# Sums between the stages of a two-layer block moved onto TensorE, and pools opened before the squares

## The chip, the cores and the metric

One core of one Trainium2 chip runs the kernel. The metric is the time of one execution on the device, in microseconds (us). TensorE is called PE here, VectorE DVE, ScalarE ACT, GpSimd POOL and SyncE SP, as the profile calls them.

## The reference

Block 1 (a delta-net and convolution mixer, a mixture of experts) makes a residual stream `x` of 512 tokens by 1024 features. Block 2 takes it through two layers; the change lies there. A layer of block 2 ends its two halves alike:

```python
    y = jnp.concatenate([y_a, y_b, y_c, y_d], axis=-1) @ w_out
    x = x + gate1 * rms_norm(y, attn_post_g)

    h = rms_norm(x, mlp_pre_g) * (1.0 + scale2) + shift2
    y = jnp.square(jax.nn.relu(h @ mlp_w1)) @ mlp_w2
    return x + gate2 * rms_norm(y, mlp_post_g)
```

So at the end of each half of a layer there is a matrix product `y`, an RMS norm of `y`, an addition to `x`, and an RMS norm of the new `x`, whose scaled copy is what the next stage multiplies with its weights. The last half of the last layer has no next stage.

## The kernel before

Tiles are stored with features on the 128 partitions (8 feature tiles, k = 0 to 7) and tokens along the free axis. Matrix products are made at nearly fp32 precision from split operands: `split` writes a high part (`wh`, `lhh`, `ffh`: a cast on ACT, L314) and a low part (`wl`, `lhl`, `ffl`: a subtraction on POOL or DVE, L315), and `mm3` multiplies wh by the high part (L343), wh by the low part (L347) and wl by the high part (L348). One output tile of 128 features over 512 tokens is 24 such matmuls.

A list scheduler orders the instructions of each engine, by the order of the program's text, by priorities and by explicit "issue after" hints. Each engine then runs its own queue strictly in that order, and tile pools decide when memory comes free.

There are four places like the one in the reference. They are called A (layer 0, attention: output projection, some 1690 to 1825 us), B (layer 0, end of the MLP, 2140 to 2210), C (layer 1, attention, 2570 to 2712) and D (layer 1, end of the MLP, 2984 to 3064.6, the end of the kernel).

At A and C the heads of the last mixer are normed (PE L1736, ACT L1737, L1739, PE L1742, a chain of small DVE instructions, ACT `hol` L1747, PE L1750, DVE L1752, POOL L1754), once for each of two tiles m0 and m1, and split. Then the output projection runs: the first four output tiles (m0 to m3) together over 512 tokens, 96 matmuls, with k outermost in the order 0, 1, 4, 5, 6, 7, 2, 3; then `halves` makes the last four tiles (m4 to m7) in two token halves of 256, called a0 to a3 and b0 to b3, 24 matmuls each. B and D use `halves` in the same way for the last four tiles of the second MLP product.

The class `Between` does what follows a place. `add(k, s)` squares an output tile (ACT L2357), squares it times the gain G (ACT L2359), multiplies output, gain and `x` (DVE L2360), and adds each of the three into an accumulator `ba` (DVE L2364). `sums` sums the accumulator over the partitions with six small fp32 matmuls (L2372; D has only one of the three sums, so two), and works out two reciprocal roots on DVE. `finish` spreads them over the partitions (PE L2391), updates `x`, and makes the next stage's split input (ACT L484 `lhh` and its low part). The sums of token half a are taken while half b still runs. That is possible because the next norm's sum is expanded into the three sums and `own_squares`, the sum of squares of the old `x`: eight squares on ACT (L2241, L2243), seven adds on POOL (L2244), four matmuls (L2247).

Before, `own_squares` has a pool of its own, `osq`, opened and closed before the pools of the output projection:

```python
        with ExitStack() as e3:
            self.own_squares(self.pool("osq", es=e3, side=here), "ab")
        ...
        hlE = self.pool("hlE", bufs=2, es=es2, side=here)
```

`hlE`, which holds the split weights of output tiles m1 and m3, lies on the memory of `osq`.

Of the kernel before, what the change touches and what calls it, by code (L numbers as in the profile page):

```python
# [9 lines left out]
F32 = mybir.dt.float32  # L10
# [4 lines left out]
AF = mybir.ActivationFunctionType  # L15
OP = mybir.AluOpType
# [4 lines left out]
P = 128  # L21
T = 512
NT = 4
D = 1024
KD = 8
TC = 256
EPS = 1e-6
# [5 lines left out]
HT = 256  # L33
# [178 lines left out]
def halves(ap, i):  # L212

    return ap.rearrange("p (t i) -> p t i", i=P)[:, HALF[i]]


class Kern:
# [123 lines left out]
    def mm3(self, out, wh, wl, xh, xl, first, last):  # L341
        mm = self.nc.tensor.matmul
        i = mm(out, wh, xh, start=first, stop=False)  # L343
        if self.behind:

            self.tc.add_manual_dep(self.behind.pop().ins, i.ins.name, mybir.DependencyInfo(mybir.DependencyClass.NoSync, mybir.DependencyReason.DATA), reason="order")
        mm(out, wh, xl, start=False, stop=False)  # L347
        mm(out, wl, xh, start=False, stop=last)  # L348

    def mtile(self, w, c0, act, n=T, m=P, tag=None, ks=range(KD)):  # L350

# [1744 lines left out]
    def layer(self, l):  # L2096

        nc, I = self.nc, self.I
        mod = self.mod2[l]
        vec = lambda n, q=8: self.V(n, l * 8, q)  # L2100
        A2, G1, G2 = (self.tab.tile([P, KD], F32, name="%s_%d" % (n, l)) for n in ("lA2", "lG1", "lG2"))
# [10 lines left out]
        here, there = ("right", None) if l else (None, "right")  # L2112
# [6 lines left out]
        for tag, side, name, gi, run in (  # L2119
# [17 lines left out]
                nc.scalar.dma_start(self.x, self.xd)  # L2137
            with ExitStack() as e3:
                run(self.pool(name, es=e3, side=side), out(gi))
        with ExitStack() as e3:  # L2140
            self.own_squares(self.pool("osq", es=e3, side=here), "ab")
        self.step_ = 1
        nc.vector.tensor_mul(G1, mod[:, 16:24], vec("attn_post_g_2"))
        nc.vector.scalar_tensor_tensor(A2, mod[:, 32:40], 1.0, vec("mlp_pre_g_2"), op0=OP.add, op1=OP.mult)
# [5 lines left out]
        self.hl, self.nhl = [self.hlC, hlE, self.hlC, hlE, self.hlC], 0  # L2150
        bd = self.pool("bd", es=es2, side=here)
        b2 = self.pool("lay4", es=es2, side=here)
        o = self.yf
        order = (0, 1, 4, 5, 6, 7, 2, 3)
        for k in order:
            self.split(self.h[0][:, k], self.h[1][:, k], self.yf[:, k])
        ws = [self.chunk(I["w_out_2"][l], j * 256, 256) for j in range(2)]
        for k, p in enumerate(self.mtiles([(w[m], 0, P, None) for w in ws for m in range(2)], self.h, ks=order)):
            nc.scalar.copy(o[:, k], p)
        ws = [self.chunk(I["w_out_2"][l], j * 256, 256) for j in range(2, 4)]  # L2160
        self.subs = (nc.gpsimd,)
        self.halves(ws, self.h, o, nc.scalar.copy, Between(self, o, G1, bd, A2, mod[:, 24:32]), order)

        if l == 0:
            ring = self.pool("mraw", bufs=1, es=es2, side=here)
# [1 line left out]
        for g in range(4):  # L2167
            if l == 0 and g == 2:
                with self.tc.issue_after(relu.ins):
                    self.own_squares(self.lay2, ("hoq", "hol"))  # L2170
            f = [[b2.tile([P, T], F32R, tag=n, name=n, bufs=8) for _ in range(KD)] for n in ("ffh", "ffl")]
            for js in ((0,), (1,), (2,), (3,)) if g else ((0, 1), (2,), (3,)):
                j = js[0]
                ws = [self.chunk(I["mlp_w1_2"][l], g * D + q * 256, 256) for q in js]
                specs = [(w[m], 0, P, None) for w in ws for m in range(2)]
                if g == 0 and j == 2:
                    self.subs = (nc.gpsimd, nc.vector)
                if g or j:
                    ps = self.mtiles(specs, self.h)
                else:  # L2180
                    ps = [self.ps() for _ in specs]
                    for s in (0, HT):
                        self.mtiles(specs, self.h, HT, o=s, ps=ps)
                for i, p in enumerate(ps):
                    r = self.lay2.tile([P, T], F32, tag="rpx", name="ffr", bufs=2)
                    relu = nc.scalar.activation(r, p, AF.Relu)
                    nc.gpsimd.tensor_mul(r, r, r)
                    self.split(f[0][2 * j + i], f[1][2 * j + i], r)
            if l == 0 and g == 0:
                self.step_ = 2  # L2190
                self.pend = self.mods(0, range(5 * D, 6 * D, P), [ring] * 8, 1) + self.mods(1, range(0, MODS_1 * 256, P), [ring] * 48, 1)
            for j in range(4 if g < 3 else 2):
                w = self.chunk(I["mlp_w2_2"][l], g * D + j * 256, 256)
                for i, p in enumerate(self.mtiles([(w[m], 0, P, None) for m in range(2)], f)):
                    k = 2 * j + i
                    if g == 0:
                        nc.scalar.copy(o[:, k], p)
                    else:
                        nc.vector.tensor_add(o[:, k], o[:, k], p)
        ws = [self.chunk(I["mlp_w2_2"][l], g * D + j * 256, 256) for j in range(2, 4)]  # L2200
# [3 lines left out]
        self.halves(ws, f, o, lambda d, p: nc.vector.tensor_add(d, d, p), Between(self, o, G2, bd, *nxt))  # L2204
        es2.close()

    def halves(self, ws, act, o, put, bt, ks=range(KD)):

        ws = [w for q in ws for w in q]

        def tile(i, s):
            p = self.ps()[:, :HT]
            for k in ks:
                x = [h[k] if isinstance(h, list) else h[:, k] for h in act]
                self.mm3(p, ws[i][0][:, k], ws[i][1][:, k], x[0][:, s], x[1][:, s], k == ks[0], k == ks[-1])
            put(o[:, 4 + i, s], p)
            bt.add(4 + i, s)

        a, b = slice(0, HT), slice(HT, T)
        for k in range(4):  # L2220
            bt.add(k, slice(0, T))
        for i in range(4):
            tile(i, a)
        for i in range(4):
            tile(i, b)
            if i == SUMS:
                bt.sums(a)
        bt.finish(a)
        bt.sums(b)
        bt.finish(b)  # L2230

# [2 lines left out]
        self.nc.vector.scalar_tensor_tensor(A, self.mod2[l][:, 8:16], 1.0, self.V("attn_pre_g_2", l * 8, 8), op0=OP.add, op1=OP.mult)  # L2234
        return A

    def own_squares(self, pool, tags):

        nc = self.nc
        acc, sq = (pool.tile([P, T], F32, tag=q, name="os" + q, bufs=1) for q in tags)  # L2240
        nc.scalar.activation(acc, self.x[:, 0], AF.Square)  # L2241
        for k in range(1, KD):
            nc.scalar.activation(sq, self.x[:, k], AF.Square)  # L2243
            nc.gpsimd.tensor_add(acc, acc, sq)  # L2244
        p = self.ps((P, NT), tag="m")
        for t in range(NT):
            nc.tensor.matmul(p[:, t:t + 1], acc[:, t * P:(t + 1) * P], self.ones1, start=True, stop=True)  # L2247
        self.sx = self.tab.tile([P, NT], F32, tag="sx", name="sx", bufs=1)
        nc.vector.tensor_scalar(self.sx, p, 1.0 / D, EPS, op0=OP.mult, op1=OP.add)

    def arrive(self):

# [88 lines left out]
class Between:  # L2341


    def __init__(self, K, o, G, pool, A=None, B=None):
        self.K, self.o, self.G, self.A, self.B, self.pool = K, o, G, A, B, pool
        self.n = 3 if A is not None else 1
        self.acc = pool.tile([P, 3, T], F32, tag="ba", name="ba", bufs=1)
        self.r = {}

    def add(self, k, s):  # L2350

        K, nc, lay, G = self.K, self.K.nc, self.K.lay2, self.G[:, k:k + 1]
        o = self.o[:, k, s]
        dst = [self.acc[:, i, s] for i in range(self.n)]
        if k:
            dst = [lay.tile([P, T], F32, tag=t, name="bs", bufs=b)[:, s] for t, b in ((("rpt", 2), ("rpt", 2), ("rpx", 2)) if k % 2 else (("hoq", 1), ("hol", 1), ("rpx", 2)))[:self.n]]
        nc.scalar.activation(dst[0], o, AF.Square)  # L2357
        if self.n > 1:
            nc.scalar.activation(dst[1], o, AF.Square, scale=G)  # L2359
            nc.vector.scalar_tensor_tensor(dst[2], o, G, K.x[:, k, s], op0=OP.mult, op1=OP.mult)  # L2360
        if k:
            for i, d in enumerate(dst):
                a = self.acc[:, i, s]
                nc.vector.tensor_add(a, a, d)  # L2364

    def sums(self, s):
        K, nc = self.K, self.K.nc
        n = HT // P
        p = K.ps((P, 3, n), tag="m")
        for i in range(self.n):  # L2370
            for t in range(n):
                m = nc.tensor.matmul(p[:, i, t:t + 1], self.acc[:, i, s.start + t * P:s.start + t * P + P], K.ones1, start=True, stop=True)  # L2372
                if s.start and not i and not t and self.A is not None:
                    K.held = [m]
        v, u = (self.pool.tile([P, n], F32, tag="b" + q, name="b" + q, bufs=2) for q in "vu")
        nc.vector.tensor_scalar(v, p[:, 0], 1.0 / D, EPS, op0=OP.mult, op1=OP.add)
        r = K.rsqrt(v, self.pool, "rm%d" % s.start)
        self.r[s.start] = [r]
        if self.A is not None:
            nc.vector.tensor_mul(u, p[:, 1], r)  # L2380
            nc.vector.scalar_tensor_tensor(u, p[:, 2], 2.0, u, op0=OP.mult, op1=OP.add)
            nc.vector.tensor_mul(u, u, r)
            nc.vector.scalar_tensor_tensor(u, u, 1.0 / D, K.sx[:, s.start // P:s.start // P + n], op0=OP.mult, op1=OP.add)
            self.r[s.start].append(K.rsqrt(u, self.pool, "rn%d" % s.start))
# [46 lines left out]
```

## Time and profile before

| | us |
|---|---|
| median of 3 runs | 3070.9 (3060.8 to 3076.36) |
| the profiled execution | 3066.41 |
| its span in the trace | 3064.6 |
| PE busy | 2738.4 (89% of the span) |
| DVE busy | 1516.2 (49%) |
| ACT busy | 934.5 (30%) |
| POOL busy | 1035.9 (34%) |

PE is busy for most of the span, and its mean granted clock is 0.92 of full speed. The four places make up a small part of the span; the change touches nothing outside them. How long something takes there is read from the timeline and the stretches, what PE waits for from the waits.

### The profile page before, as it was taken

The page shows a single profiled execution, that of the slowest core. Times are in us where ns is not written, and L with a number is a line of the kernel's source. Part 1 is how long each engine was busy: PE and PEld are TensorE (multiplying, and loading weights), DVE is VectorE, ACT ScalarE, POOL GpSimd, SP SyncE. Part 2 cuts the span into 40 slices and gives each one's busy share as a digit, 9 for nine tenths or more (in the row PEclk, how much of TensorE's full clock was granted, in tenths as well). Part 3 has the DMA queues.
Part 4 walks back from the last instruction along what each step waited for, and adds up shares of the span by engine and source line. Part 5 has one row for each costly group of instructions (what it writes and reads, how often), then busy time and mean ns, then how long its engine had stood idle before and what let it go on. Part 6 is the DMA issues. An engine that isn't in the chain of part 4 may idle for free.

```text
span 3064.6 us, 43712 instructions
## 1 busy us (share of the span) xinstructions
PE 2738.4 (89%) x17212; PEld 2025.5 (66%) x17218; DVE 1516.2 (49%) x3330; ACT 934.5 (30%) x1842; POOL 1035.9 (34%) x793
## 2 busy tenths in 40 slices
PE   7999998988999988579988889999989989899997
PEld 5767887645456443456666777878855657788886
DVE  4877766432121111458666475653748474632224
ACT  4243334211111111234333342323334233433221
POOL 3324423012222222252332354544243242454432
PEclk8989898999999999689898899999899898899998
DMA  5134003689999999311042225552211041222221
GB/s 216 43 118 152 28 6 111 252 293 388 356 373 357 361 366 376 106 70 56 29 145 89 88 71 188 169 170 93 74 55 42 30 149 42 83 83 95 92 91 53
DMA packets 81358, 456.55 MB, mean 149 GB/s; under 512 B 12272, under 2 KB 19088, under 8 KB 34944
## 3 DMA queue, kind: packets, MB, share of 16 engines
q1 hardware_dynamic: 64224, 411.27, 36.5%
q0 software_dynamic: 11280, 27.80, 3.8%
q10 hardware_dynamic: 5648, 14.68, 1.3%
q8 instruction: 136, 2.23, 0.3%
q14 instruction: 70, 0.57, 0.1%
HBM read 434.82 MB, written 27.26 MB: 151 GB/s over the span
## 4 chain that ended last, share of the span: by engine, by line
PE 35%; DVE 9%; DMA 3%; POOL 2%; ACT 2%; issue 2%; DVEq 0%; ACTq 0%; POOLq 0%
PE ps_pj L347 5%; PE ps_pj L343 5%; PE ps_pj L348 5%; PE ps_a L347 4%; PE ps_a L343 4%; PE ps_a L348 4%; DMA rawm<-in_mod_w_dram 3%; DVE rawm L401 2%; PE ps_a L1727 1%; DVE ba L2364 1%; PE ps_m L1979 1%; PE ps_a L2062 1%; PE ps_a L1717 1%; PE ps_a L1750 1%; PE ps_a L1848 1%
## 5 line engine op out<-in xcount | busy, mean ns | idle before, releaser
L315 POOL TENSOR_TENSOR wl<-raw,wh 128x1024 fp32r<-128x1024 f32 (+1 forms) x161 | 392.8, 2442 | 719.6 <-ACT wh L314 673.3
L314 ACT CAST wh<-raw 128x1024 fp32r<-128x1024 f32 (+1 forms) x235 | 240.6, 1034 | 499.5 <-PE ps_a L347 344.3
L343 PE MATMUL ps_pj<-lhh,wh 128*128 128x512 f32 (+5 forms) x816 | 327.6, 402 | 0.6 <-ACT a_wi L1777 0.6
L348 PE MATMUL ps_pj<-lhh,wl 128*128 128x512 f32 (+5 forms) x816 | 316.7, 388 | 5.7 <-POOL wl L315 5.7
L347 PE MATMUL ps_pj<-lhl,wh 128*128 128x512 f32 (+5 forms) x816 | 316.7, 388 | 0.0
L315 DVE TENSOR_TENSOR wl<-raw,wh 128x1024 fp32r<-128x1024 f32 x74 | 127.3, 1721 | 207.0 <-ACT wh L314 207.0
L401 DVE SCALAR_TENSOR_TENSOR rawm<-rawm,cb 128x1024 f32<-128x1024 f32 x112 | 172.2, 1554 | 108.7 <-DMA rawm<-in_mod_w_dram 89.6
L1331 POOL DMA_INDIRECT yrows<-ey,ssrc x60 | 85.2, 1421 | 347.1 <-DMA yrows<-ey,ssrc 190.0
L343 PEld LDWEIGHTS ps_pj<-lhh,wh 128*128 128x128 f32 (+2 forms) x816 | 160.7, 197 | 40.7 <-issue 12.3
L348 PEld LDWEIGHTS ps_pj<-lhh,wl 128*128 128x128 f32 (+2 forms) x816 | 159.8, 196 | 39.1 <-POOL wl L315 7.4
L347 PEld LDWEIGHTS ps_pj<-lhl,wh 128*128 128x128 f32 (+2 forms) x816 | 160.4, 197 | 36.5 <-issue 10.0
L343 PE MATMUL ps_a<-lhh,wh 128*128 128x512 f32 (+3 forms) x464 | 167.5, 366 | 18.1 <-ACT lhh L484 13.1
L1304 PE MATMUL ps_c<-raw,xT 128*128 128x256 f32 (+3 forms) x704 | 168.9, 396 | 5.5 <-DMA raw<-in_experts_dram 5.5
L1308 DVE SCALAR_TENSOR_TENSOR eh<-eh,swt,ps_c 64x256 f32<-64x256 f32 (+7 forms) x50 | 23.7, 474 | 294.4 <-ACT eh L1306 294.4
L348 PE MATMUL ps_a<-lhh,wl 128*128 128x512 f32 (+3 forms) x464 | 166.6, 360 | 2.3 <-DVE wl L315 2.3
L347 PE MATMUL ps_a<-lhl,wh 128*128 128x512 f32 (+3 forms) x464 | 167.3, 361 | 0.7 <-POOL lhl L488 0.5
L1299 PE MATMUL ps_c<-raw,xT 128*32 128x256 f32 (+4 forms) x1408 | 140.1, 403 | 27.4 <-DMA raw<-in_experts_dram 27.4
L1304 PEld LDWEIGHTS ps_c<-raw,xT 128*128 128x128 f32 (+3 forms) x704 | 120.7, 176 | 46.0 <-issue 8.0
L1299 PEld LDWEIGHTS ps_c<-raw,xT 128*32 128x32 f32 (+4 forms) x1408 | 72.4, 124 | 90.6 <-DMA raw<-in_experts_dram 32.3
L1306 ACT ACTIVATE eh<-ps_c 64x256 f32<-64x256 f32 (+7 forms) x56 | 21.4, 382 | 334.6 <-PE ps_c L1304 198.2
L347 PE MATMUL ps_a<-ffl,wh 128*128 128x512 f32 (+1 forms) x288 | 107.2, 372 | 13.1 <-DVE ffl L315 13.1
L343 PEld LDWEIGHTS ps_a<-lhh,wh 128*128 128x128 f32 x464 | 93.9, 205 | 30.8 <-ACT lhh L484 14.7
(851 smaller groups left out, 6177.2 us busy)
## 6 DMA issues: line engine op xcount, KB each, us to landing
raw<-in_experts_dram SPq DMA_DIRECT2D x192, 1024.0 KB, 24.6
raw<-in_mlp_w_dram SPq DMA_DIRECT2D x64, 1024.0 KB, 4.8
raw<-in_w_in_dram SPq DMA_DIRECT2D x38, 1024.0 KB, 4.8
rawm<-in_mod_w_dram SPq DMA_DIRECT2D x28, 1024.0 KB, 4.9
rawm<-in_mod_w_dram SPq DMA_DIRECT2D x40, 512.0 KB, 3.7
raw<-in_w_out_dram SPq DMA_DIRECT2D x12, 1024.0 KB, 5.0
rawm<-in_w_mod_dram SPq DMA_DIRECT2D x20, 512.0 KB, 3.6
raw<-in_w_mod_dram SPq DMA_DIRECT2D x8, 1024.0 KB, 18.7
```

What stands on the lines that cost most here:

```text
L314: self.nc.scalar.copy(hi, src)
L315: (eng or self.sub_engine()).tensor_sub(lo, src, hi.bitcast(F32))
L343: i = mm(out, wh, xh, start=first, stop=False)
L347: mm(out, wh, xl, start=False, stop=False)
L348: mm(out, wl, xh, start=False, stop=last)
L401: self.nc.vector.scalar_tensor_tensor(raw[:, m], raw[:, m], 1.0, cb, op0=OP.mult, op1=OP.mult, accum_out=out[:, m:m + 1])
L1299: self.last_mm = mm(pg[c:c + n, :256], xT[:, k, 32 * q:32 * q + n], w[i][:, k], start=k == 0, stop=k == KD - 1, **at(c))
L1304: self.last_mm = mm(o, xT[:, k], w[:, k], start=k == 0, stop=k == KD - 1)
L1331: nc.gpsimd.indirect_dma_start(out=self.yrows, out_offset=bass.IndirectOffsetOnAxis(ap=r, axis=0), in_=y[c], in_offset=None, bounds_check= ...
L1717: nc.tensor.transpose(p[:, j], e[:, j * P:(j + 1) * P], self.ident)
L1727: self.nc.tensor.matmul(p[64 * q:64 * q + 64], v[:, j, cols[q]], pts[q][:, j], start=j == 0, stop=j == t)
L1750: nc.tensor.matmul(b[:, t * P:(t + 1) * P], l[:, t], self.ident, start=True, stop=True)
```

## The change

Two things are changed.

First, the pools of the output projection are opened before `own_squares`, which no longer has a pool: its two tiles are taken from the `ffh` and `ffl` buffers of the MLP's pool. Its squares and adds stand later in the program, and its four matmuls are issued inside `halves`, after tile a3.

Second, `Between` loses the accumulator, the DVE adds into it and the second ACT square. For each k there is one square on ACT and, at A, B and C, one product on DVE. PE sums them: each 128 x 128 piece of the square is the stationary operand against two columns (1 and G squared), each piece of the product against one column of ones, and PSUM accumulates over k. A place has 64 such matmuls (32 at D) instead of 12 (4 at D). They wait in a list, `todo`, and are issued one output tile later (`some`). Squares and products take turns through three pairs of buffers by k modulo 3. The last four (2 at D) come after `finish` of half a; at A, B and C they are spread through the next stage's first matmuls.

```diff
+            self.tiled = self.last3
             put(o[:, 4 + i, s], p)
             bt.add(4 + i, s)

         a, b = slice(0, HT), slice(HT, T)
+
         for k in range(4):
             bt.add(k, slice(0, T))
         for i in range(4):
             tile(i, a)
+            bt.some(self.tiled, 2)
+        if first:
+            with self.tc.issue_after(self.tiled.ins):
+                first()
         for i in range(4):
             tile(i, b)
+            if len(bt.todo) > 1:
+                bt.some(self.tiled, len(bt.todo) - 1 if i < 1 else 1)
             if i == SUMS:
                 bt.sums(a)
         bt.finish(a)
+        bt.some(None)
         bt.sums(b)
         bt.finish(b)
...
-        with ExitStack() as e3:
-            self.own_squares(self.pool("osq", es=e3, side=here), "ab")
...
         b2 = self.pool("lay4", es=es2, side=here)
+        own = self.own_squares(b2, ("ffh", "ffl"), 8)
...
-        dst = [self.acc[:, i, s] for i in range(self.n)]
-        if k:
-            dst = [lay.tile([P, T], F32, tag=t, name="bs", bufs=b)[:, s] for t, b in ((("rpt", 2), ("rpt", 2), ("rpx", 2)) if k % 2 else (("hoq", 1), ("hol", 1), ("rpx", 2)))[:self.n]]
-        nc.scalar.activation(dst[0], o, AF.Square)
+        q, (tag, bufs) = ((lay, ("rpt", 2)), (lay, ("rpx", 2)), (self.pool, ("bs", 2)))[k % 3]
+        tile = lambda: q.tile([P, T], F32, tag=tag, name="bs", bufs=bufs)[:, s]
+        sq = tile()
+        nc.scalar.activation(sq, o, AF.Square)
+        what = [(sq, self.gg[:, k] if self.n > 1 else K.ones1, slice(0, min(self.n, 2)))]
         if self.n > 1:
-            nc.scalar.activation(dst[1], o, AF.Square, scale=G)
-            nc.vector.scalar_tensor_tensor(dst[2], o, G, K.x[:, k, s], op0=OP.mult, op1=OP.mult)
-        if k:
-            for i, d in enumerate(dst):
-                a = self.acc[:, i, s]
-                nc.vector.tensor_add(a, a, d)
+            d = tile()
+            nc.vector.scalar_tensor_tensor(d, o, G, K.x[:, k, s], op0=OP.mult, op1=OP.mult)
+            what.append((d, K.ones1, slice(2, 3)))
+
+        def products():
+            hold = []
+            for a in range(s.start, s.stop, P):
+                h = a // HT * HT
+                new = h not in self.p
+                if new:
+                    self.p[h] = K.ps((P, HT // P, 3), tag="m")
+                for i, (src, col, c) in enumerate(what):
+                    hold.append(nc.tensor.matmul(self.p[h][:, (a - h) // P, c], src[:, a - s.start:a - s.start + P], col, start=new and not i,
+                                                 stop=k == KD - 1 and a + P == h + HT and i == len(what) - 1))
+            if s.start and k == KD - 1 and self.A is not None:
+                K.held = hold[::-1]
+
+        self.todo.append(products)
+
+    def some(self, after, n=1):
+
+        with self.K.tc.issue_after(after.ins) if after else ExitStack():
+            for _ in range(n):
+                self.todo.pop(0)()
```

What that does to the queues is shown at three spots. PE at A, before, from the end of the last mixer: the small matmuls of the head norms (L1750, L1736, L1742) and of the squares (L2247, of the accumulator `osa`) stand ahead of the first output-projection matmul.

```order
L1905 MATMUL ps_m<-b_s,b_v 64x128 x8
L1750 MATMUL ps_a<-const_all,hol 128x128 x4
L1736 MATMUL ps_a<-yf,const_two 128x512
L1742 MATMUL ps_a<-const_two,hoq 128x2 x4
L2247 MATMUL ps_m<-const_all,osa 128x1 x4
L1750 MATMUL ps_a<-const_all,hol 128x128 x4
L1736 MATMUL ps_a<-yf,const_two 128x512
L343 MATMUL ps_pj<-lhh,wh 128x512
```

PE at A, after, the same spot:

```order
L1905 MATMUL ps_m<-b_s,b_v 64x128 x8
L343 MATMUL ps_pj<-lhh,wh 128x512
L347 MATMUL ps_pj<-lhl,wh 128x512
L348 MATMUL ps_pj<-lhh,wl 128x512
L343 MATMUL ps_pj<-lhh,wh 128x512
L1750 MATMUL ps_a<-const_all,hol 128x128 x4
L1736 MATMUL ps_a<-yf,const_two 128x512
```

Four projection matmuls now stand ahead of L1750; 8 more follow L1736 ahead of m0's L1742, then 16 ahead of m0's L1750, 8 ahead of m1's L1742 and 6 ahead of m1's L1750, so that 54 of the 96 are left behind the last L1750, where there were 78 before. L2247 (now L2257) is gone from here.

ACT at A, before: the squares of `x` (`osb`) stand among the head norms, and the casts of `wh` behind them.

```order
L2243 ACTIVATE osb<-xres 128x512
L1739 ACTIVATE hoq<-yf 128x512
L2243 ACTIVATE osb<-xres 128x512 x2
L1747 COPY hol<-rq_y 128x512
L314 CAST wh<-raw 128x1024 x2
L1737 COPY yf<-ps_a 128x512
```

ACT at A, after, from the last cast of `hoq` for m1 on: the squares (`osffh`, `osffl`) stand behind the head norms, and the cast of `wh` for m5 behind the squares.

```order
L1739 ACTIVATE hoq<-yf 128x512
L1747 COPY hol<-rq_y 128x512
L2249 ACTIVATE osffh<-xres 128x512
L2251 ACTIVATE osffl<-xres 128x512
L314 CAST lhh<-yf 128x512
L2251 ACTIVATE osffl<-xres 128x512 x6
L314 CAST wh<-raw 128x1024
L2158 COPY yf<-ps_a 128x512
```

On POOL the seven adds of the squares (L2252) follow both L1754 and stand ahead of the `wl` of m5, in the same way.

PE at D, after, the end of the program: between the matmuls of tile b3 and the two spreads there are two products on either side; before, only the two of L2372 stood there.

```order
L348 MATMUL ps_pj<-ffh,wl 128x256
L2390 MATMUL ps_m<-const_all,bs 128x1 x2
L2423 MATMUL ps_m<-const_all,rq_y 128x128 x2
L2390 MATMUL ps_m<-const_all,bs 128x1 x2
L2423 MATMUL ps_m<-const_all,rq_y 128x128 x2
```

In all D has 30 products ahead of its first spread, where two matmuls stood before; A, B and C have 60 where six stood, in the order: 16 with a1 (A, C) or ahead of it (B), another 16, then 8, 4, 4, 4, 4 and 4 with the tiles after.

## Rows read from the trace of the kernel before

**Rows 1.** The page: busy time (share of the span), instructions of PE.

```profile
PE 2738.4 (89%) x17212; PEld 2025.5 (66%) x17218; DVE 1516.2 (49%) x3330; ACT 934.5 (30%) x1842; POOL 1035.9 (34%) x793
```

**Rows 2.** Stretches: length, busy per engine (instructions), granted clock, DMA share, GB/s.

```profile
1726.00:1733.00 7.00, 7.00 (x24) 5.94 (x24) 1.71 (x11) 1.56 (x2) 0.00 (x0) 0.52 0.64 228
1733.00:1751.00 18.00, 18.00 (x81) 14.71 (x80) 2.34 (x3) 2.65 (x5) 4.40 (x3) 1.00 0.00 0
1774.00:1781.00 7.00, 7.00 (x35) 7.00 (x35) 6.62 (x22) 1.44 (x3) 1.94 (x1) 0.51 0.22 89
2183.00:2207.00 24.00, 23.80 (x110) 23.43 (x110) 17.60 (x60) 7.38 (x17) 8.69 (x11) 0.50 0.00 1
2655.00:2661.00 6.00, 5.74 (x27) 5.75 (x28) 5.79 (x16) 1.73 (x4) 2.36 (x1) 0.50 0.39 158
3016.00:3040.00 24.00, 24.00 (x202) 23.91 (x201) 11.82 (x30) 4.86 (x10) 2.40 (x1) 1.00 0.00 1
1284.00:1291.00 7.00, 6.84 (x32) 6.84 (x33) 3.74 (x18) 4.24 (x10) 2.18 (x1) 0.50 0.27 107
```

**Rows 3.** Waits of PE at A, 1700 to 1812: total, times, longest us.

```profile
PE ps_m L2247 <- POOL osa L2244: 4.2, 1, 4.2
PE ps_m L2391 <- DVE rq_y L386: 4.0, 1, 4.0
PE ps_a L1742 <- ACT hoq L1739: 3.4, 1, 3.4
PE ps_m L2372 <- DVE ba L2364: 3.2, 1, 3.2
PE ps_pj L348 <- POOL wl L315: 1.5, 1, 1.5
PE ps_a L348 <- DVE wl L315: 1.1, 1, 1.1
```

**Rows 4.** Timeline of PE at A: start, us, instruction; a group of sums.

```profile
1798.52 1.39 PE L2372 MATMUL ps_m<-const_all,ba 128*128 128x1 f32 x12
1799.78 0.37 PE L347 MATMUL ps_a<-lhl,wh 128*128 128x256 f32 x1
```

**Rows 5.** Timelines of POOL, ACT and PE at A, in brackets idle before.

```profile
1715.09 1.26 POOL L2244 TENSOR_TENSOR osa<-osa,osb 128x512 f32<-128x512 f32 x1 [0.74 <-ACT osb L2243]
1718.36 1.99 ACT L314 CAST wh<-raw 128x1024 fp32r<-128x1024 f32 x2 [1.33 <-PE ps_m L2247]
1731.81 1.65 PE L1750 MATMUL ps_a<-const_all,hol 128*128 128x128 f32 x8
1734.41 2.20 POOL L1754 TENSOR_TENSOR yf<-yf,b_gate 128x512 f32<-128x512 f32 x1 [9.00 <-DVE yf L1752]
1750.10 2.40 POOL L315 TENSOR_TENSOR wl<-raw,wh 128x1024 fp32r<-128x1024 f32 x1 [11.46 <-ACT wh L314]
```

**Rows 6.** Timeline of PE at B, from the last tile on.

```profile
2174.46 0.28 PE L348 MATMUL ps_pj<-ffh,wl 128*128 128x256 f32 x1
2179.49 0.71 PE L2391 MATMUL ps_m<-const_all,rq_y 128*128 128x128 f32 x4 [2.78 <-DVE rq_y L386]
2182.62 0.69 PE L343 MATMUL ps_a<-lhh,wh 128*128 128x256 f32 x2 [2.43 <-ACT lhh L484]
```

**Rows 7.** Waits of PE at C, 2600 to 2694: total, times, longest us.

```profile
PE ps_a L343 <- ACT lhh L484: 5.9, 2, 3.8
PE ps_m L2391 <- DVE rq_y L386: 4.5, 1, 4.5
PE ps_pj L348 <- POOL wl L315: 1.6, 2, 1.3
```

**Rows 8.** Timeline of PE at C: the sums of half a.

```profile
2655.26 2.72 PE L2372 MATMUL ps_m<-const_all,ba 128*128 128x1 f32 x12 [3.21 <-DVE ba L2364]
```

**Rows 9.** Timeline of DVE at D, among the last updates of half a.

```profile
3040.87 0.43 DVE L2364 TENSOR_TENSOR ba<-ba,bs 128x256 f32<-128x256 f32 x1
```

**Rows 10.** Timeline of PE in the step between the blocks: squares against two columns.

```profile
1284.16 3.15 PE L2278 MATMUL ps_a<-vog,vq 128*128 128x2 f32 x14 [5.10 <-DVE vu L2285]
```

More of the change, by code (lines that the diff above doesn't have):

```diff
@@ L347, in mm3 @@
         mm(out, wh, xl, start=False, stop=False)
-        mm(out, wl, xh, start=False, stop=last)
+        self.last3 = mm(out, wl, xh, start=False, stop=last)
     def mtile(self, w, c0, act, n=T, m=P, tag=None, ks=range(KD)):
@@ L2161, in layer @@
         self.subs = (nc.gpsimd,)
-        self.halves(ws, self.h, o, nc.scalar.copy, Between(self, o, G1, bd, A2, mod[:, 24:32]), order)
+        self.halves(ws, self.h, o, nc.scalar.copy, Between(self, o, G1, bd, A2, mod[:, 24:32]), order, own)
         if l == 0:
@@ L2169, in layer @@
                 with self.tc.issue_after(relu.ins):
-                    self.own_squares(self.lay2, ("hoq", "hol"))
+                    self.own_squares(self.lay2, ("hoq", "hol"))()
             f = [[b2.tile([P, T], F32R, tag=n, name=n, bufs=8) for _ in range(KD)] for n in ("ffh", "ffl")]
@@ L2205, in layer, with halves @@
         es2.close()
-    def halves(self, ws, act, o, put, bt, ks=range(KD)):
+    def halves(self, ws, act, o, put, bt, ks=range(KD), first=None):
         ws = [w for q in ws for w in q]
@@ L2235, in first_scale, with own_squares @@
         return A
-    def own_squares(self, pool, tags):
+    def own_squares(self, pool, tags, bufs=1):
         nc = self.nc
-        acc, sq = (pool.tile([P, T], F32, tag=q, name="os" + q, bufs=1) for q in tags)
+        acc, sq = (pool.tile([P, T], F32, tag=q, name="os" + q, bufs=bufs) for q in tags)
         nc.scalar.activation(acc, self.x[:, 0], AF.Square)
@@ L2244, in own_squares, with rest @@
             nc.gpsimd.tensor_add(acc, acc, sq)
[L2245 to L2249, printed above, removed]
+        def rest():
+            p = self.ps((P, NT), tag="m")
+            for t in range(NT):
+                nc.tensor.matmul(p[:, t:t + 1], acc[:, t * P:(t + 1) * P], self.ones1, start=True, stop=True)
+            self.sx = self.tab.tile([P, NT], F32, tag="sx", name="sx", bufs=1)
+            nc.vector.tensor_scalar(self.sx, p, 1.0 / D, EPS, op0=OP.mult, op1=OP.add)
+        return rest
     def arrive(self):
@@ L2346, in __init__ @@
         self.n = 3 if A is not None else 1
-        self.acc = pool.tile([P, 3, T], F32, tag="ba", name="ba", bufs=1)
+        if self.n > 1:
+            self.gg = pool.tile([P, KD, 2], F32, tag="bg", name="bg", bufs=1)
+            K.nc.vector.memset(self.gg[:, :, 0], 1.0)
+            K.nc.vector.tensor_mul(self.gg[:, :, 1], G, G)
+        self.p = {}
+        self.todo = []
         self.r = {}
@@ L2368, in sums @@
         n = HT // P
[L2369 to L2374, printed above, removed]
+        p = self.p[s.start].rearrange("p t i -> p i t")
         v, u = (self.pool.tile([P, n], F32, tag="b" + q, name="b" + q, bufs=2) for q in "vu")
```

## The prediction

> **What bounds the kernel now.** The page first: PE is busy for 89% of the span [rows 1], so what is added to PE's queue lengthens the kernel unless it falls into a gap of PE, and what is taken from DVE, ACT or POOL helps only where PE waits for it. The stretches come next, for the price of a matmul and for the clock: 0.222 us for one of 512 tokens at full clock (18.00 us over 81), 0.119 for one of 256 (24.00 over 202), both with PE busy without a break; and several stretches at half clock, 1.2 GHz, in which PE is as fully busy but does less [rows 2]. The third view is what PE waits for. At A these are the norm of the heads (L1742 for `hoq`, 3.4), the squares of `x` (L2247, 4.2), a `wl` (1.5, and 1.1 in the halves), the accumulator (L2372, 3.2) and the reciprocal root (L2391, 4.0) [rows 3]. C has the same kinds, 3.2 and 4.5 in the tail [rows 7, 8]; B has waits after its halves only [rows 6]; at D PE never waits inside the halves [rows 2]. So removing DVE adds can pay at A and C, little at B, and nothing at D.
>
> **The price of the new sums.** The old sums have the same shape: a 128 x 128 fp32 tile as stationary operand against one column. Twelve passes, which are six matmuls, took 1.26 us from their start to the start of the next matmul [rows 4], 0.21 per matmul at full clock. A second column costs nothing that a row shows: fourteen passes with two columns took 3.15 us at half clock [rows 10], 0.225 each, twice the 0.105 of the one-column passes. A, B and C get 60 matmuls ahead of half a's spread in place of 6: 54 x 0.21 = **+11.3** each. D gets 30 in place of 2: 28 x 0.21 = +5.9. None of it is hidden where PE has no gap.
>
> **A.** Head: the casts of `wh` for m1 and m3 waited for L2247 [rows 5], as their pool lay on the squares' memory. With the pools opened first they go early, projection matmuls fill PE between the head norms, and `hoq` no longer queues behind squares. The waits of 3.4, 4.2 and 1.5 go, 9.1 in all. Given back: with only 6 projection matmuls behind m1's L1742 (1.4 us), the DVE chain and the copy `hol` behind it are covered in part, about 1.3, and at m0 a `wl` on DVE stands in that chain, about 0.7. So -7.1. Some of the projection's matmuls that ran at half clock from 1726 to 1733 [rows 2] may then run at full clock, which is worth up to 3.5; I take -1.9. Head: -9, between -5 and -11.
>
> First halves: here the removed wait comes back in part. The squares now stand on ACT ahead of the cast of `wh` for m5, their adds on POOL ahead of its `wl`, and the first add stands behind m1's L1754. One step of that ping-pong takes 2.0 us (an add of 1.26 after 0.74 of waiting [rows 5]). From the end of L1754 there are the first add, 1.3, an `lhl`, 1.2, six more adds, 11.3, and the `wl`, 2.4: m5's weights are there 16.2 later. L1754 started 2.6 after L1750 [rows 5] and took 2.20 while DVE worked on a `wl`; alone I give it 1.3 as the adds, so its end is 3.9 behind L1750. PE does L1750 (1.3), 54 x 0.222 = 12.0 and a0 (24 x 0.119 = 2.9) in 16.2 and stands at a1 12.3 after L1754's end: a wait of about 3.9. Then the first products need squares and DVE products that stand behind copies, two more casts and a `wl`: another 1 to 2. Against that goes the 1.1 that was there. First halves: **+4**, from 0 (the adds run ahead) to +6.
>
> Tail: the accumulator is gone (-3.2); half a's sums are ready some tiles earlier, since DVE has no adds in front of the root, so the wait of 4.0 goes; and the 7 us at half clock that followed the first wait [rows 2] lost 3.5. Tail: -10.7. What is late next is the first update of the next stage (`lhh`), which stays, as the spread at the end of b3 starts it. A: -9 + 4 + 11.3 - 10.7 = **-4.4**.
>
> **B.** +11.3. From the last matmul's start to the next stage's first there are 8.2 us [rows 6], with two spreads one after the other and waits ahead of and behind them. With the root done early both spreads run together and one wait of some 3 us for `lhh` is left: -3.5. B: **+7.8**. Behind it lie 24 us at half clock with PE busy throughout [rows 2]; I let that stand, since one wait stays.
>
> **C.** Head: the wait for `wl` (1.6 [rows 7]) and a little filling, -2. First halves +4 for the same reason as at A. Products +11.3. Tail: -3.2 and -4.5 [rows 7, 8], and 6 us at half clock [rows 2] lost 3: -10.7. C: **+2.6**.
>
> **D.** +5.9, and the last add of DVE among the updates, 0.43 [rows 9], goes: **+5.5**. Nothing hides it: the halves are PE without a gap, and the chain after them is as long as before.
>
> **The sum.** -4.4 + 7.8 + 2.6 + 5.5 = +11.5. Less 1 for the waits of the next stage's second half behind A and C, which a lighter DVE should shorten. The new wait in a1 is of the size of the old ones that were followed by 7 and 6 us at half clock [rows 2], a loss of 3.5 and 3; I count half of it, +3.3. Together **+13.8**: 3080.2 against the profiled execution's 3066.41, and 3084.7 against the median of 3070.9, which lies 4.5 above it. I put the time between them, at 3082.
>
> **The rivals.**
>
> *The clock falls in the product groups.* In the step between the blocks PE was busy 6.84 of 7 us with two-column products and small matmuls, and the clock stayed at 0.50 [rows 2, 10]. At A, B and C 16 products stand in a row (3.4 us), then 24 matmuls, then up to 16 more. If the clock falls there, 32 products at 0.45 cost 7 more and a1's matmuls 2.2: +9 a place, 27 in all, or +24 beyond what is counted: 3104. With two of three places it is about +16: 3096 to 3098. Against it: groups of 12 passes ran at full clock on both sides of them [rows 4]. The Trainium skill, in Part 1 of "TensorE: Matmul & The Clock Gate", says that the halved clock is the idle state and activity releases it; by that rule the busy product groups would hold full clock and this rival would be nothing. The stretch of [rows 10], busy and at 0.50, speaks against reading it so, and I keep the rival. Chance 0.21.
>
> *The first part doesn't do what it says.* The early projection matmuls may find their operands late: the weights of m4 and m5 are loaded only when a `wl` has freed the raw tile, and m4's cast stands ahead of `hol` on ACT. Then the head gains about nothing at A (+9): 3089 to 3093. Chance 0.13.
>
> *Faster.* The squares run ahead, so a1 waits nowhere (-8, and -3.3 of clock); the head gains its 11 (-2); and as B reaches the next stage with one wait, its 24 us at half clock [rows 2] run at full clock (-12). The waits for `lhh` at C [rows 7], 5.9, shrink by 5. Then 13.8 - 30.3 = -16.5, which is 3050 to 3054. It decides at B: only if the clock stays up behind the spread does the kernel get faster. For it: of the 8.2 us there 3.5 go. Against it: single waits of 3.2 were followed by half clock at A and C [rows 2]. Chance 0.15.
>
> The forecast itself has 0.51, nearly all of it between 3072 and 3091.
>
> **The chances.** 0.5% is 15 us, about what a measurement of this kernel tells from no change. The forecast lies just inside it, with some of its own spread above: same 0.46, slower 0.40 (clock, head, and the upper edge of the forecast), faster 0.14. The range reaches from the faster rival to the clock rival: 3050 to 3102.
>
> **What would show it.** PE at D should be longer by 28 small matmuls, 5 to 6 us, with no new wait; if D is not longer, the price is wrong. L2247's and L1742's waits at A should be gone, and a wait of 3 to 5 us on `wl` should stand in a1 of A and C; if it doesn't, the squares ran ahead. L2372's and L2391's waits should be gone at A and C. At B the halves should take about 36 us in place of 24. The clock of a1 and a2 at B tells the first rival from the forecast: B has no new wait there. The prediction is wrong if products cost less than 0.15 among the matmuls, or if the stretch behind B changes its clock.

## The result, and the profile after

| | before | after |
|---|---|---|
| median us | 3062.46 (8 runs, 3055.76 to 3076.36) | 3089.45 (8 runs, 3086.05 to 3092.5) |
| span of the trace | 3064.6 | 3084.3 |
| PE busy | 2738.4 | 2776.1 |
| DVE busy | 1516.2 | 1457.8 |

The changed kernel is slower by 0.93%: the ratio is 1.0093, with a 95% interval of 1.007 to 1.0117, some 27 us by the medians. The page's line that answers to [rows 1] has the added work in it: PE gained 374 instructions and 37.7 us, DVE lost 58.4 us, and the kernel follows PE.

```profile
PE 2776.1 (90%) x17586; PEld 2061.4 (67%) x17586; DVE 1457.8 (47%) x3226; ACT 918.9 (30%) x1806; POOL 1031.1 (33%) x793
```

The two spans differ by 19.7 and not by 27. If the start of the same matmul is compared in both traces, the trace of before loses 9 us to that of after up to 1530 and another 9.6 up to 1690, in stretches whose PE instructions stand in the same order in both. Some of the latter is half clock that only the one run had. Between B and C it is the trace of after that loses 3.7. So the places are compared by themselves: from a matmul ahead of a place to one behind it, A got longer by 3.1, B by 11.2, C by 12.8 and D by 6.4 us, some 33 in all.

The waits of PE at A, from 1682 to 1800 of the changed kernel (total, times, longest us), answer to [rows 3]. The waits for the squares, for the accumulator and for the root are gone; that for `hoq` has fallen from 3.4 to 0.7; in their place stand `wl`, `wh`, the operands of the products (`bs`) and, in the last mixer, `b_s`.

```profile
PE ps_a L343 <- ACT lhh L484: 3.6, 2, 1.8
PE ps_m L1905 <- DVE b_s L1900: 3.3, 1, 3.3
PE ps_pj L348 <- POOL wl L315: 2.2, 1, 2.2
PE ps_a L1750 <- ACT hol L1747: 1.2, 1, 1.2
PE ps_m L2390 <- ACT bs L2375: 1.1, 1, 1.1
PE ps_m L2390 <- DVE bs L2379: 0.9, 2, 0.7
PE ps_a L1742 <- ACT hoq L1739: 0.7, 1, 0.7
PE ps_pj L343 <- ACT wh L314: 0.6, 1, 0.6
```

The wait for `b_s` is new, and the prediction did not have it. With the pools open early, POOL makes two `wl` at the very time at which DVE works on the norm of the heads, ahead of that `b_s`. Two DVE instructions on 128 x 8 values, which took 0.17 each before, take 2.27 and 2.26, and end with the two `wl` (first line before, the others after):

```profile
1699.72 0.17 DVE L376 TENSOR_SCALAR rq_y<-rq_b 128x8 int32<-128x8 int32 x1
1681.33 4.65 POOL L315 TENSOR_TENSOR wl<-raw,wh 128x1024 fp32r<-128x1024 f32 x2 [25.32 <-ACT wh L314]
1681.43 2.27 DVE L376 TENSOR_SCALAR rq_y<-rq_b 128x8 int32<-128x8 int32 x1
1683.74 2.26 DVE L377 TENSOR_TENSOR rq_t<-rq_y 128x8 f32<-128x8 f32 x1
```

All kernels below that have the first part show this wait, at 3.0 to 3.6; the one without that part has 0.7 there.

The wait for `wl` comes from where the prediction put it. POOL adds the squares of `x` at one add in 2.03 us (1.29, and 0.74 of waiting for ACT's next square), and the `wl` of m5 stands behind the last:

```profile
1722.61 1.29 POOL L2252 TENSOR_TENSOR osffh<-osffh,osffl 128x512 f32<-128x512 f32 x1 [0.74 <-ACT osffl L2251]
1724.64 1.27 POOL L2252 TENSOR_TENSOR osffh<-osffh,osffl 128x512 f32<-128x512 f32 x1 [0.74 <-ACT osffl L2251]
1725.88 2.34 POOL L315 TENSOR_TENSOR wl<-raw,wh 128x1024 fp32r<-128x1024 f32 x1
```

What the waits don't show, the stretches do (length, busy time per engine, granted clock, DMA share, GB/s). The first three are B's halves; then the first halves at A and at C; then D.

```profile
2136.00:2142.00 6.00, 6.00 (x56) 6.00 (x55) 5.29 (x6) 2.26 (x4) 2.40 (x1) 1.00 0.41 128
2142.00:2156.00 14.00, 14.00 (x82) 14.00 (x82) 1.39 (x3) 0.83 (x2) 0.00 (x0) 0.63 0.05 21
2156.00:2177.00 21.00, 21.00 (x183) 21.00 (x182) 11.20 (x39) 4.40 (x8) 0.00 (x0) 1.00 0.13 41
1729.00:1742.00 13.00, 11.38 (x51) 11.09 (x52) 5.99 (x6) 4.15 (x8) 4.81 (x2) 0.50 0.49 163
2641.00:2654.00 13.00, 12.04 (x55) 11.75 (x55) 5.33 (x5) 3.66 (x8) 4.56 (x2) 0.50 0.43 155
3030.00:3057.00 27.00, 27.00 (x233) 26.91 (x232) 5.80 (x20) 4.79 (x10) 2.41 (x1) 1.00 0.00 1
```

At B, PE is busy for 14.00 of 14 us, waits for nothing, and the clock is granted at 0.63 on the mean: it falls to 1.2 GHz behind the first 16 products and again within the next 16. At A and C the first halves run at half clock for 13 us, and the clock falls once more behind the next 16 products. From a0 to b0 the granted clock is at half for 17.1 us at A, 10.2 at B and 17.1 at C, where the kernel before has none; half of that, 22 us, is lost. D, with eight products at the most in a row, keeps full clock. There the price of one product can be read: eight (sixteen passes) from 3033.20 to the start of the next matmul at 3034.90, 0.2125 each, which answers to [rows 4].

```profile
3033.20 1.84 PE L2390 MATMUL ps_m<-const_all,bs 128*128 128x1 f32 x16
3034.90 0.36 PE L343 MATMUL ps_pj<-ffh,wh 128*128 128x256 f32 x1
```

### The profile page after: what moved, and what is told of

It is laid out like the page before. It is cut to its first block, busy times and chain, and to the rows that moved or that the text cites. A ratio compares the mean times of both kernels' runs of the same rounds, so it can differ in the third digit from the quotient of the medians.

```text
span 3084.3 us, 44280 instructions
## 1 busy us (share of the span) xinstructions
PE 2776.1 (90%) x17586; PEld 2061.4 (67%) x17586; DVE 1457.8 (47%) x3226; ACT 918.9 (30%) x1806; POOL 1031.1 (33%) x793
## 4 chain that ended last, share of the span: by engine, by line
PE 37%; DVE 7%; DMA 3%; POOL 2%; ACT 2%; issue 2%; ACTq 0%; DVEq 0%; POOLq 0%
PE ps_pj L343 5%; PE ps_pj L347 5%; PE ps_pj L348 5%; PE ps_a L347 4%; PE ps_a L343 4%; PE ps_a L348 4%; DMA rawm<-in_mod_w_dram 3%; DVE rawm L401 2%; PE ps_m L2390 2%; PE ps_a L1727 1%; PE ps_m L1979 1%; PE ps_a L2062 1%; PE ps_a L1750 1%; PE ps_a L1717 1%; PE ps_m L1905 1%
## 5 line engine op out<-in xcount | busy, mean ns | idle before, releaser
L343 PEld LDWEIGHTS ps_pj<-lhh,wh 128*128 128x128 f32 (+2 forms) x816 | 161.4, 198 | 41.1 <-issue 13.4
L1306 ACT ACTIVATE eh<-ps_c 64x256 f32<-64x256 f32 (+7 forms) x56 | 21.3, 380 | 324.2 <-PE ps_c L1304 191.4
## 6 DMA issues: line engine op xcount, KB each, us to landing
raw<-in_experts_dram SPq DMA_DIRECT2D x192, 1024.0 KB, 24.9
raw<-in_w_mod_dram SPq DMA_DIRECT2D x8, 1024.0 KB, 18.7
```

## The experiments

Theory 1: the loss is the products on PE, their bare price and the half clock that they bring. Theory 2: it is the first part, whose squares of `x` hold up m5's weights, with the half clock behind that wait.

For all kernels the same three steps are worked out from the traces, at A and at C: how far the start of a0 is shifted against before, measured from the same matmul ahead of the place (1690 and 2572 of the trace before); how long a0 to the start of b0 takes; and how long from there to the first matmul of the next stage. At B only the last two. All in us.

| kernel | A: a0, a half, rest | B: a half, rest | C: a0, a half, rest |
|---|---|---|---|
| before | 0, 12.8, 29.3 | 11.4, 20.7 | 0, 12.9, 29.3 |
| after | -11.0, 33.9, 21.5 | 25.6, 18.5 | +1.4, 32.7, 21.5 |
| pools alone | -11.0, 19.3, 29.0 | 11.4, 21.3 | -2.0, 18.7, 28.6 |
| sums alone | -1.8, 30.9, 21.0 | 25.5, 18.5 | +2.9, 31.0, 21.1 |
| spread | -11.2, 41.1, 22.1 | 20.2, 19.3 | -2.1, 39.9, 22.4 |
| squares written later | -10.9, 39.6, 21.5 | 25.6, 18.5 | -2.1, 37.0, 21.5 |
| adds on DVE | -11.0, 31.0, 21.5 | 25.6, 18.5 | -2.0, 29.3, 21.5 |
| pools, adds on DVE | -10.9, 13.7, 28.7 | 11.4, 20.8 | -2.1, 13.7, 28.4 |
| one pass | -10.9, 26.2, 20.5 | 16.2, 16.7 | +1.4, 24.9, 20.5 |

**Each part alone.** In the first kernel `Between` is the old class, and the rest is as after the change:

```diff
-        self.halves(ws, self.h, o, nc.scalar.copy, Between(self, o, G1, bd, A2, mod[:, 24:32]), order, own)
+        self.halves(ws, self.h, o, nc.scalar.copy, Added(self, o, G1, bd, A2, mod[:, 24:32]), order, own)
```

(`Added` is `Between` of before; the same is done at B and D.)

> The first part alone: the pools open first, the squares of x stand late, and the sums between stages are the old ones (accumulator on DVE, twelve and four small matmuls). Theory 1 (the loss of the changed kernel is the products on PE, at 0.23 us each and with half-clock stretches around them): the head of A gains about 10 us, a1 gives back 3 to 5 at A and C, so the kernel is 0 to 10 us faster than before. Theory 2 (the loss is the squares that now stand ahead of m5's weights, with the wait and the half clock behind it): 5 to 12 us slower than before.

Measured: 0.9989 of before (0.9973 to 1.0005). In the second kernel the squares stand in their own pool, ahead of the others:

```diff
+        with ExitStack() as e3:
+            self.own_squares(self.pool("osq", es=e3, side=here), "ab")()
...
-        own = self.own_squares(b2, ("ffh", "ffl"), 8)
...
```

> The second part alone: the sums on PE, but the squares of x keep their own pool ahead of the others, as before. Theory 1: 25 to 35 us slower than before, the whole of the changed kernel's loss or more, with half clock at B's product groups and in the halves of A and C. Theory 2: 10 to 18 us slower, the bare price of the products less the waits that go, with the clock full in the halves of A and C.

Measured: 1.0096 (1.0071 to 1.0122), as slow as both parts together. Theory 2 falls: the first part by itself costs nothing. But in the first kernel its gain is paid back on the spot. There a0 starts 11.0 earlier at A, and a0 to b0 takes 6.5 longer, with the same wait for `wl` and no product. The waits of PE at A in the first kernel, two of them:

```profile
PE ps_pj L348 <- POOL wl L315: 2.2, 1, 2.2
PE ps_pj L343 <- ACT wh L314: 1.4, 1, 1.4
```

In the same kernel the half clock behind that wait is short (0.57 over 4 us, some 3.4 us at half) and the clock soon back; so the wait alone starts a stretch at half clock, but does not make the 13 us of it:

```profile
1732.00:1736.00 4.00, 3.70 (x18) 3.71 (x19) 4.00 (x4) 4.00 (x7) 2.81 (x2) 0.57 0.70 229
1736.00:1752.00 16.00, 13.32 (x110) 12.92 (x109) 16.00 (x23) 8.97 (x21) 6.11 (x3) 1.00 0.21 76
```

**The products in another order.** The products of half a are cut by 128 tokens and issued behind each k of the next tile:

```diff
+                if bt.drip:
+                    with self.tc.issue_after(self.last3.ins):
+                        bt.drip.pop(0)()
...
-            bt.some(self.tiled, 2)
+            bt.drip += bt.todo.pop(0).parts + bt.todo.pop(0).parts
```

> The changed kernel, but the products of half a don't stand in groups of 16, 8 and 4 behind a tile: two go behind each k of the next tile, that is two products behind three matmuls. Their number and work are the same. If the groups turn the clock down (theory 1), the clock stays full through B's halves and these take 35.5 to 36.5 us in place of 40.6; the kernel is 5 to 12 us faster than the changed one. If it is the small matmuls themselves, wherever they stand, B's halves stay at 40 us or get slower.

Measured: 1.0132 (1.0106 to 1.0158), slower than the changed kernel, against the expectation; the places say why. B did what theory 1 says: the half a takes 20.2 in place of 25.6, at full clock (the first line below). A and C got slower by 7 each: 34 us at half clock, with PE busy for more than 32 of them (the second and third).

```profile
2163.00:2181.00 18.00, 18.00 (x157) 18.00 (x158) 7.05 (x34) 2.70 (x6) 0.00 (x0) 1.00 0.00 1
1736.00:1770.00 34.00, 32.43 (x153) 32.14 (x153) 6.48 (x8) 5.39 (x12) 4.76 (x2) 0.51 0.16 59
2647.00:2681.00 34.00, 32.88 (x155) 32.58 (x155) 6.16 (x8) 5.21 (x12) 4.11 (x2) 0.50 0.15 57
```

The same mixture, two products behind three matmuls, kept the clock that it met: full at B, where PE came without a wait, half at A and C, where it came from the wait in a1. With groups of 16 it fell even at B, and came back in the unbroken tiles between them.

**The wait in a1 taken away.** The first try wrote `own_squares` further down, behind the weights of m4 to m7:

```diff
-        own = self.own_squares(b2, ("ffh", "ffl"), 8)
...
         self.subs = (nc.gpsimd,)
+        own = self.own_squares(b2, ("ffh", "ffl"), 8)
```

> The changed kernel, but the squares of x are written behind the weights of m4 to m7, so that they stand behind m5's cast on ACT and its subtraction on POOL. The wait for wl in a1 (2.2 at A, 1.8 at C) goes. Theory 2: with it the half clock in a1 to a2 goes at A and C, and the kernel is 8 to 14 us faster than the changed one. Theory 1: the products still turn the clock down at A and C, as they do at B without a wait, and it is 3 to 6 us faster.

Measured: 1.0136 (1.0107 to 1.0164), and the edit missed its purpose. The scheduler still puts the squares ahead of m5's cast; why is not shown. In this kernel the last square on ACT starts at 1728.94, the cast behind it, and `wl` was waited for as before (2.2). So it separates nothing. Half a got 5.7 longer at A and 4.3 at C, as the half clock in it lasted 27.3 and 23.9 us in place of 17.1 at both. The second try takes the ping-pong away: a tile for each square, and the adds on DVE.

```diff
+            if bufs > 1 and k > 1:
+                sq = pool.tile([P, T], F32, tag=tags[1], name="os" + tags[1], bufs=bufs)
             nc.scalar.activation(sq, self.x[:, k], AF.Square)
-            nc.gpsimd.tensor_add(acc, acc, sq)
+            (nc.vector if bufs > 1 else nc.gpsimd).tensor_add(acc, acc, sq)
```

> The changed kernel, but the squares of x at A and C go into tiles of their own and are added on DVE, so that neither m5's cast on ACT nor its subtraction on POOL stands behind the ping-pong. The wait for wl in a1 goes (2.2 at A, 1.8 at C). Theory 2 (the wait starts the half clock there): full clock through a1 and a2, 10 to 16 us faster than the changed kernel. Theory 1 (the products do it, as at B): some 7 to 14 us of half clock stay at A and C, 4 to 8 us faster.

Measured: 1.008 (1.0064 to 1.0096). The waits for `wl` and `wh` are gone at A; A's and C's first halves are shorter by 2.9 and 3.4, less than theory 2 wants, and the half clock stays, with PE busy for every microsecond of it (second line). Ahead of it PE still waits, for the products' own operands (first line; the longer of the two waits ends at 1731.69, 1.2 ahead of the fall):

```profile
PE ps_m L2392 <- DVE bs L2381: 1.7, 2, 1.5
1733.00:1750.00 17.00, 17.00 (x81) 17.00 (x82) 1.72 (x3) 3.04 (x6) 2.36 (x1) 0.50 0.12 52
```

So at A the clock falls without a wait for `wl`. That the products alone would bring it down there, without a wait for their operands, is not shown; at B, where no wait is near, it is.

**The first part with its wait taken away.** The old sums, and the edit above.

> The first part alone with the old sums, and the squares of x added on DVE. If the first part's gain at the head of A and C is real and only the ping-pong takes it back, this is 6 to 14 us faster than before; if the gain is given back elsewhere (the accumulator's and the root's waits on DVE grow by what the halves win), within 4 us of the first part alone, which was 3 us faster than before.

Measured: 0.9962 (0.9942 to 0.9981), 10 us faster than before by the medians and faster than both kernels. By place A gains 10.1, the others nothing: at A the start of a0 is 10.9 earlier and only 0.9 is paid back in the first half. At C the next stage starts 2.1 earlier and loses this again behind its first matmuls, in stretches at half clock that the trace of before has not; the wait for the root, at 4.5 before [rows 7], is still there, at 4.8.

**One pass in place of two.** Squares, products and columns as fp32r; the number of matmuls is the same, and each has two columns.

```diff
-        tile = lambda: q.tile([P, T], F32, tag=tag, name="bs", bufs=bufs)[:, s]
+        tile = lambda: q.tile([P, T], F32R, tag=tag, name="bs", bufs=bufs)[:, s]
...
-            what.append((d, K.ones1, slice(2, 3)))
+            what.append((d, self.on, slice(2, 4)))
```

> The changed kernel, but squares and products are written as fp32r and the columns too (two columns each), so that each product is one pass on PE in place of two. The number of matmuls is the same. Theory 1 (the passes are the price): some 6 us less at A, B and C each and 3 at D, more where the half clock gets shorter: 18 to 28 us faster than the changed kernel. If the price were the queueing of small matmuls or their waits, it moves by less than 8.

Measured: 1.0005 (0.9995 to 1.0016): 27 us of the changed kernel's loss are gone. A product takes 0.11 us, the distance of the starts here, and B runs its halves at full clock, 16.2 for half a (the 0.99 comes from a fall at 2159.55, behind the halves):

```profile
2131.29 0.25 PE L2394 MATMUL ps_m<-bg,bs 128*128 128x2 f32 x1
2131.40 0.25 PE L2394 MATMUL ps_m<-bon,bs 128*128 128x2 f32 x1
...
2127.00:2160.00 33.00, 30.57 (x262) 30.38 (x261) 20.09 (x54) 8.15 (x15) 3.13 (x2) 0.99 0.17 58
```

This is the clearest of the runs for theory 1: the same matmuls and order, nearly the same waits (0.6, 2.2, 1.1 and 1.1 at A), half the passes. Half a at B got shorter by 9.5: 44 products at 0.10 less are 4.4, and the 10.2 us at half clock that are gone are worth 5.1.

**D by itself.** The old accumulator at D alone.

```diff
-        self.halves(ws, f, o, lambda d, p: nc.vector.tensor_add(d, d, p), Between(self, o, G2, bd, *nxt))
+        self.halves(ws, f, o, lambda d, p: nc.vector.tensor_add(d, d, p), (Added if l else Between)(self, o, G2, bd, *nxt))
```

> The changed kernel with the old accumulator and sums at D alone. Theory 1 (each product costs its passes on PE, and nothing hides them): D shrinks by the 6 us that the traces show there, A, B and C stay; 5 to 7 us faster than the changed kernel. If D's products were hidden by its DVE chain, the time would not move.

Measured: 1.0108 (1.009 to 1.0126). The times cannot tell it from the changed kernel, whose interval overlaps. The trace can: from the same matmul, some 120 us ahead of D's halves, to the end it takes what it took before, where the changed kernel takes 6.4 longer. The 6 us are D's, but the total did not confirm it.

**All three.** One pass at A, B and C, the old sums at D, the adds on DVE.

> Three edits together: the products as fp32r (one pass each) at A, B and C, the old accumulator at D, and the squares of x added on DVE. Per place, from the traces of the single edits: A -9 (a one-pass halves' stretch without the wait for wl), B -1, C -3 to 0, D 0. Theory 1: 9 to 14 us faster than before, about as the pools with old sums and adds on DVE (-10 to -12), since the sums' work is then small either way. If the edits don't add up (the half clock in A's and C's halves stays with one pass), 3 to 6 us faster.

Measured: 0.9963 (0.9944 to 0.9982), the same as the first part with adds on DVE. Half a at A still takes 24.6, with the clock at 0.67 on the mean over 21 us:

```profile
1729.00:1750.00 21.00, 19.28 (x111) 19.00 (x111) 8.10 (x8) 5.16 (x11) 4.67 (x2) 0.67 0.26 96
```

## Why the prediction was right, and where not

The time lies in the range and on the forecast side, but at its slower part: 0.9% where the likeliest case was 0.45%, and beyond what I had as the likeliest class, within 0.5%. As a difference, 13.8 us were forecast and 27 measured. Two things helped: the range reached up to the price of the clock rival, and the eight runs of the kernel before have their median 8.4 below the 3070.9 that the forecast was added to, so that 3082 looks nearer to 3089 than it is. By its steps:

- **What bounds the kernel.** Right: 58 us less on DVE paid only in the tails at A, B and C, where PE had waited, and the kernel is slower for what PE got.
- **The price of a product**, 0.21. Right: 0.21 at D, and 0.22 at B, where two columns and one take turns. In the fp32r kernel, with half the passes, it is 0.11, which shows that it is the passes.
- **A's head**, -9. Measured -11.0, the edge that was given, but made up otherwise. Ahead of a0 the kernel before is at half clock for some 24 us and the changed one for some 10 (means of 0.80 and 0.90 in the first two lines below), worth 7 where 1.9 was counted. That leaves 4 for the waits, where 7.1 was forecast: the new wait for `b_s`, 3.3, took the rest. The number came near by luck.
- **C's head**, -2. The changed kernel got +1.4; of the eight other kernels with the first part six got -2.0 or -2.1, one -5.0 and one +1.4. The half clock ahead of a0 tells them apart: some 17 us before, 20 in the two with +1.4, 14 in the six (the last line shows one) and 7 in the one with -5.0. With half of the difference taken off, all nine lie within 0.4 of the kernel before: the head at C gained nothing. Here too a wait for `b_s` grew, from 0.6 to 2.4.

```profile
1690.00:1751.10 61.10, 50.67 (x244) 41.61 (x243) 18.20 (x46) 17.89 (x31) 20.48 (x14) 0.80 0.22 78
1671.80:1721.90 50.10, 43.45 (x235) 35.06 (x235) 16.26 (x46) 14.53 (x25) 16.15 (x11) 0.90 0.26 95
2572.00:2633.20 61.20, 57.58 (x306) 46.93 (x304) 21.85 (x58) 21.19 (x39) 24.46 (x16) 0.86 0.11 42
2572.00:2634.50 62.50, 59.68 (x296) 46.16 (x295) 22.58 (x56) 19.18 (x34) 20.13 (x14) 0.84 0.11 40
2554.43:2613.60 59.17, 55.67 (x297) 42.98 (x296) 22.45 (x56) 18.54 (x33) 19.49 (x13) 0.88 0.12 43
```

- **The wait in a1.** Right in its cause (the ping-pong of squares, at 2.03 a step where 2.0 was worked out) and in size: 0.6, 2.2, 1.1 and 0.7 make 4.6, less the 1.1 of before, where +4 was forecast.
- **The tails.** Right. The waits for the accumulator and the root are gone. From b0 to the next stage A and C take 7.8 less; the forecast was 10.7 less, with 16 products in place of six (2.1) to pay. At B it was 2.2 less, where 3.5 less and the same 2.1 more were forecast. Behind B, where the prediction let the half clock stand and named a change of it as a sign of being wrong, it did change: the mean is 0.59 from 2180.35 to 2204.35, for the 24 us at 0.50 of [rows 2], which is worth 2.
- **D**, +5.5. Measured +6.4, of it 5.7 from the start of a0 on.
- **The clock.** This is the term that was mis-sized. I counted +3.3 for A and C together and nothing for B, and left the rest to a rival with a chance of 0.21. Half a got longer by 21.1 at A, 14.3 at B and 19.8 at C. Of that 44 products at 0.2125 are 9.4 each, and the waits 3.5 at A and 2.4 at C. What remains is 8.2, 4.9 and 8.0: **21 us** in place of 3.3, as the granted clock has it (22). What the wait in a1 brings by itself was counted right: the kernel with the pools alone has 3.4 us at half clock in half a at A and at C, 1.7 lost at each. What the products add was left to the rival. It had 9 for each place, 27 in all, so it came close in price. In mechanism too, but for one thing: at B the first 16 products themselves ran at full clock, and the tile behind them paid. It was kept small because groups of 12 passes ran at full clock on both sides in [rows 4]; behind the 32 passes at B the clock fell.

The rule of the Trainium skill that stood beside the rival (in "TensorE: Matmul & The Clock Gate", Part 1, activity releases the halved clock) does not help to forecast this, if busy time in the profile is taken for activity: PE was busy for 14.00 of 14 us at B, and its clock fell. The measurement decides.

Two things stay open. One is why some half clock stays in A's half a with one-pass products, while B has none: the products and their waits for squares stand together there and were not separated. The other is why stretches at half clock differ in length between kernels whose PE order is the same there, as at C's head, or in half a between the changed kernel (17.1) and the one with the squares written later (27.3).

## What to carry to other kernels

A reduction over partitions with the data as stationary operand cost PE 0.106 us for each pass here, though only one column comes out, where a matmul of 256 columns costs 0.119. Before moving such sums to a busy PE, count the passes, halve them with fp32r where the precision allows, and look what the clock does in a row of them. An order that frees one engine's wait can put a chain of two other engines in front of the next operand: read what stands behind the moved instructions on each queue, and give a ping-pong more buffers. Work that an early buffer lets POOL start can meet DVE's short instructions: look at their durations too.

## What the runs showed of the hardware that was not expected

- DVE instructions on 128 x 8 values took 2.27 and 2.26 us in place of 0.17 while POOL made two `wl` of 128 x 1024, and PE waited 3.3 us for what stood behind them.
- PE at 14.00 of 14 us busy can lose its full clock, from 2.4 to 1.2 GHz: at B behind 16 products (32 passes with one or two columns), with no wait near. With eight in a row at D, and with 16 single passes at B in the fp32r kernel, it kept 1.00 and 0.99.
- A mixture of two products and three matmuls of 256 columns kept either level for as long as it ran: 1.00 for 18 us at B, 0.50 to 0.51 for 34 us at A and C, in the same kernel.
